# The scan of a bidirectional RWKV-7 mixer on one core: inverse loads and row stores go to GpSimd's queue, low parts to GpSimd

## The chip, the core and the metric

The kernel runs on one core of a Trainium2 chip. Its time is the device time of one launch in microseconds (us). The kernel before took 1601.57 us (median of 3 runs, 1601.06 to 1603.18). A core has TensorE (PE in the profile, with its weight loads as PEld), VectorE (DVE), ScalarE (ACT), GpSimd (POOL) and SyncE (SP), each working through its own instructions in order. DMA transfers are issued as instructions of SP, ACT or POOL; a transfer that waits for its data holds whatever stands behind it on the engine that issues it.

## The reference

One layer over 128 context tokens and 2048 latent tokens, width 1024. What matters for the change:

```python
h = _rmsnorm(x, lp['norm_g']) * (1.0 + scale) + shift
proj = h @ lp['w_in']
r, k, v, g_a, b_gate, c_gate, u_conv, g_b = jnp.split(proj, IN_SPLITS, axis=-1)
...
def step(S, inp):                      # per token, per direction, per head
    r_t, w_t, k_t, v_t, kk_t, a_t = inp
    s_kk = jnp.einsum('bdhij,bdhj->bdhi', S, kk_t)
    S = (S * w_t[..., None, :] - s_kk[..., :, None] * (kk_t * a_t)[..., None, :]
         + v_t[..., :, None] * k_t[..., None, :])
    return S, jnp.einsum('bdhij,bdhj->bdhi', S, r_t)
...
ya = ya.astype(x.dtype) * jax.nn.silu(g_a)                                        # group A: the scan
yb = b_gate * _short_conv(c_gate * u_conv, lp['conv_w'], is_latent) * jax.nn.silu(g_b)   # group B
u = jnp.concatenate([ya, yb], axis=-1) @ lp['w_out']
return x + gate * u, s_final           # then a last RMS norm
```

## The kernel before

There are three phases. Phase 1 projects the tokens in blocks of 384 and leaves per-token operands of the scan in scratch arrays in HBM (`at`, `lo`, `ops`, `vt`, `q`, `sg`, and `mixT`, the transposed input of the output projection, whose lower half is group B's result). Phase 2 is the scan. Phase 3 is the output projection with the last norm; part of its work, the products of group B with the output weights, is used to fill TensorE during the scan.

**The scan.** A chunk has 64 tokens. A *stage* is 8 chunks of a head pair in each of the two directions; there are 17 stages, number 0 to 16. For each stage the delta rule needs inverses of 32x32 triangles. They are made by GpSimd: `load_I` (L947) fetches the triangles from `at` with four transfers of 128 KB (L956) into a tile `ab`, of which there are two; `solve_steps` (L963) does the elimination in 15 steps of one multiplication (L978, into `ztmp`) and two subtractions (L981, into `zt`), after a preparation (L970 `dgp`, L971, L973, L974), and stores the result in `zt` in HBM (L986), from where the stage fetches it as `zc` (L1058). Stages 0 to 5 are solved before the main loop begins; the main loop's round s computes stage s, prepares stage s + 1 and asks for the solve of stage s + 7 (`partI`, L1354). GpSimd so makes the inverses of stages 6 to 16 one after the other during the scan.

**The other work in a round.** `finish` (L1209) normalises a head pair of 512 tokens once both directions are summed, gates it and writes it into 128 rows of `mixT` (L1262; L1260 for the context): the *mixed rows*. `conv_weights` (L1415) fetches the output weights of group B, and `split` (L1407) cuts each into a high part (ScalarE, L1409) and a low part, the difference (L1410); the low part is `wol`. `conv_split` (L1442) does the same for a tile of 128 tokens of group B (`mhc`; its low part is the second half of the tile, two tiles exist). `fill` (L1466) multiplies these on TensorE for nine of the 17 token tiles (`AHEAD`), half a tile of 512 columns per round, four groups of three products: high by high, high by low weight, low mix by high weight. The sums stand in the one PSUM tile `psa`, are copied by ScalarE to a tile `z0` (L1475) and stored in HBM (L1476): the *added products*, which phase 3 fetches again. The tile `z0` has one buffer, and so has `psa`:

```python
z = O.r.tile([128, 512], F32, tag="z0", name=f"z0_{i}{h}", bufs=1)
P.copy(z[:], ps[:])
```

so the copy of one half cannot begin before the store of the half before it has landed, and the products of the half after cannot begin before the copy is done.

**What sets the order.** The rounds' order on TensorE is written out by hand (`ORDER`, L758) and pinned product by product. Everything else is placed by the framework's scheduler, which estimates when each instruction could run and writes one fixed order for each engine; on the chip an engine follows that order, and waits at an instruction until its semaphores are reached. `behind` (L848) adds an order without a wait. `O.line` is true from the start of the main loop until its last round.

Of the kernel before, what the change touches and what calls it, by code (L numbers as in the profile page):

```python
# [36 lines left out]
def place(d, h):  # L37

    x = 1 - h if d == 0 else h
    return slice(x * 64, x * 64 + 64)  # L40
# [721 lines left out]
def phase2(K):  # L762
    nc, tc, A, S = K.nc, K.tc, K.A, K.S
    V, G, P, T = nc.vector, nc.gpsimd, nc.scalar, nc.tensor
    D = nc.sync.dma_start
    B = Ctx()
    O = Ctx()
# [32 lines left out]
    def spare(name, dt, tag, n=1024):  # L800

        pool = O.rI if tag in ("ab", "zt", "ztmp") else O.l1 if tag in ("ab2", "a1", "a2", "o10", "o11") else O.r0
        return pool.tile([128, n], dt, tag=tag, name=name, bufs=dict(F=4, zt=2).get(tag, 1))
# [29 lines left out]
    def ps_tile(shape, name):  # L833

        O.n += 1
        if O.pm is None and O.p2 is None:
            return K.rest_tile(name)
        if O.pm is not None and (O.n % 5 < 2 or O.p2 is None):
            return O.pm.tile(shape, F32, tag="m", name=name)
        return O.p2.tile(shape, F32, tag="s", name=name)  # L840
# [7 lines left out]
    def behind(r, ins):  # L848

        if ins is not None:  # L850
            tc.add_manual_dep(r.ins, ins.name, mybir.DependencyInfo(mybir.DependencyClass.NoSync, mybir.DependencyReason.DATA), reason="order")
# [13 lines left out]
    def now(r):  # L865
        if O.line:
            behind(r, O.last)

    def scaled(r):
        if O.line:  # L870
            behind(r, O.scaled)

    def tr(dst, src, one, after):
        r = T.transpose(dst, src, one)
        if O.line:
            behind(r, O.last)
            O.last = r.ins
        else:
            behind(r, after)

    def tl(shape, tag, b, pool=None, dt=F32):
        return (pool or O.l0).tile(shape, dt, tag=tag, name=f"{tag}_{K.u()}", bufs=b)
# [64 lines left out]
    def load_I(s, ab, after):  # L947

        for gi, (d, units, blk) in enumerate(stages[s]):
            for h in range(2):  # L950
                dst = ab[h * 64 + gi * 32:h * 64 + gi * 32 + 32].rearrange("p j i -> p (j i)")
                if blk is None:
                    src = S["at"][d, :, 0:2].rearrange("p u s b j i -> p (u s b) (j i)")
                else:
                    src = S["at"][d, units[0][0], units[0][1]:units[0][1] + 8].rearrange("u s b j i -> (u s b) (j i)")
                behind(D(dst, src), after)  # L956

    def solve(*a):

# [249 lines left out]
    def finish(p, blk, y):  # L1209

        t0 = NCTX + 512 * blk if blk is not None else 0
        other = p == 3 and blk in (2, 3)
        place = lambda tag: spare(f"{tag}{K.u()}", F32, "ztmp" if tag == "sg" else "zt", 512) if other else tl([128, 512], tag, 1)
        sg, q = place("sg"), place("yo")
        if blk is None:
            parts = [(pp_, slice(pp_ * 128, pp_ * 128 + 128)) for pp_ in range(4)]
        else:
            parts = [(p, slice(0, 512))]

        def fetch(nm, t_):  # L1220
            if blk is None:
                D(t_[:].rearrange("p (g t) -> p g t", t=128), S[nm][:, 0:128].rearrange("(g p) t -> p g t", p=128))
            else:
                now(D(t_[:], S[nm][p * 128:(p + 1) * 128, t0:t0 + 512]))

        fetch("sg", sg)
        fetch("q", q)
        yield
        heads = lambda x: x.rearrange("p q (h v) -> p (q h) v", h=2)
        per_head = lambda x: x[:].unsqueeze(2).broadcast_to((128, 8, 64))  # L1230
        if blk is None:
            mn = tl([128, 8], "ymn", 1)
            V.tensor_reduce(mn[:], heads(y[:]), mybir.AxisListType.X, ALU.add)
            V.scalar_tensor_tensor(heads(y[:]), per_head(mn), -1.0 / 64, heads(y[:]), ALU.mult, ALU.add)
        w = place("w")
        w4 = w[:].rearrange("p (q v) -> p q v", q=4)
        now(P.activation(w4, y[:], AF.Square))
        yield
        ss = tl([128, 8], "yss", 2)
        scaled(V.tensor_reduce(ss[:], heads(w4), mybir.AxisListType.X, ALU.add))  # L1240
        P.activation(ss[:], ss[:], AF.Sqrt, bias=B.geps[:], scale=1.0 / 64)
        yield
        V.reciprocal(ss[:], ss[:])
        V.tensor_tensor(heads(y[:]), heads(y[:]), per_head(ss), ALU.mult)
        yield
        pt = ps_tile([128, 512], f"psT{K.u()}")
        for i in range(4):
            if blk is None:
                dst = pt[:, i * 128:i * 128 + 128]
            else:  # L1250
                dst = pt[:].rearrange("p (m q t) -> p m q t", m=2, q=4)[:, :, i]
            tr(dst, y[:, i], B.idt[:], K.reached)
        yield
        o = y[:].rearrange("p q t -> p (q t)")
        for g_, cs in parts:
            scaled(V.scalar_tensor_tensor(o[:, cs], pt[:, cs], B.gwh[:, g_:g_ + 1], sg[:, cs], ALU.mult, ALU.mult))
        yield
        scaled(V.tensor_tensor(o, o, q[:], ALU.add))
        if blk is None:
            D(S["mixT"][0:512, 0:128].rearrange("(g p) t -> p g t", p=128), o.rearrange("p (g t) -> p g t", t=128))  # L1260
        else:
            D(S["mixT"][p * 128:(p + 1) * 128, t0:t0 + 512], o)  # L1262
        K.mixed[blk] = K.mixed.get(blk, 0) + 1
        yield

# [130 lines left out]
def phase3(K):  # L1396
    nc, tc, A, S = K.nc, K.tc, K.A, K.S
    V, G, P, T = nc.vector, nc.gpsimd, nc.scalar, nc.tensor
    D = nc.sync.dma_start
    O = Ctx()  # L1400
# [3 lines left out]
    HALF = [slice(0, 512), slice(512, 1024)]  # L1404
    wk, ready, cm, am = {}, {}, {}, {}

    def split(hi, lo, raw, eng, at=K_NOW):  # L1407

        at(K, P.copy(hi, raw))  # L1409
        at(K, eng.tensor_tensor(lo, raw, hi.bitcast(F32), ALU.subtract))  # L1410
# [4 lines left out]
    def conv_weights():  # L1415
        raw = {}

        def load(k):
            raw[k] = O.r.tile([128, 1024], F32, tag="mhc", name=f"woraw{k}", bufs=2)
            for c in HALF:  # L1420
                K.now(D(raw[k][:, c], A["wout"][k * 128:(k + 1) * 128, c]))
                yield

        def cut(k):
            t = [O.r.tile([128, 1024], F32R, name=f"wo{x}{k}") for x in "hl"]
            wk[k] = [[x[:, c] for c in HALF] for x in t]
            for n, c in enumerate(HALF):
                split(wk[k][0][n], wk[k][1][n], raw[k][:, c], V)
                yield

        k0, k1, k2, k3 = CONV
        for step in (load(k0), load(k1), cut(k0), load(k2), cut(k1), load(k3), cut(k2), cut(k3)):
            yield from step
# [8 lines left out]
    def conv_split(i, at=K_NOW):  # L1442
        raw = cm[i]
        t = O.r.tile([128, 1024], F32R, tag="mhc", name=f"mhc{i}", bufs=2)
        cm[i] = [t[:, c] for c in HALF]
        split(*cm[i], raw[:], V, at)

    def mixes():
        for i in AHEAD:
# [5 lines left out]
    def product(ps, m, ks, h, n, start, stop, pin=lambda r: None):  # L1455

        hi, lo = m
        wh, wl = [x[h] for x in wk[ks[n]]]
        c = slice(n * 128, n * 128 + 128)
        for x, (l, r) in enumerate(((hi, wh), (hi, wl), (lo, wh))):  # L1460
            r = T.matmul(ps[:], l[:, c], r, start=start and n == x == 0, stop=stop and n == 3 and x == 2)  # L1461
            O.first = O.first or r.ins
            K.reached = r.ins
            pin(r)

    def fill():  # L1466

        for i in AHEAD:
            for h in range(2):
                ps = K.fill_tile(f"psa{i}_{h}")  # L1470
                for n in range(4):
                    product(ps, cm[i], CONV, h, n, True, True, K.pin)
                    if n == 3:
                        z = O.r.tile([128, 512], F32, tag="z0", name=f"z0_{i}{h}", bufs=1)
                        P.copy(z[:], ps[:])  # L1475
                        P.dma_start(S["z0"][i, :, HALF[h]], z[:])  # L1476
                    yield

    def att_weights():
# [127 lines left out]

    O.first = K.reached = None
    K.weights, K.conv_weights, K.mixes, K.fill, K.att_weights, K.first_mixes, K.tail = weights, conv_weights, mixes, fill, att_weights, first_mixes, tail
    K.open_rest, K.rest_tile, K.close_rest = open_rest, rest_tile, close_rest  # L1610

# [48 lines left out]
```

## Time and profile before

| | |
|---|---|
| time, median of 3 runs | 1601.57 us (1601.06 to 1603.18) |
| the profiled execution's own time | 1599.22 us |
| its span, first to last instruction | 1597.2 us |
| the main loop of the scan in it, about | 1010 to 1440 us |
| DMA issues on POOL's queue in all | 15 (L986) |
| DMA issues on SP's queue in all | 991 |

The profile comes from one execution; its times count from the span's start. "Busy" leaves out waiting and the issuing of DMAs by SP and ACT; a DMA issue on POOL is a row of its own with a duration. The idle time before an instruction is put down to what released it last. Of a DMA the profile has the issue and the landing.

### The profile page before, as it was taken

The page shows a single profiled execution, that of the slowest core. Times are in us where ns is not written, and L with a number is a line of the kernel's source. Part 1 is how long each engine was busy: PE and PEld are TensorE (multiplying, and loading weights), DVE is VectorE, ACT ScalarE, POOL GpSimd, SP SyncE. Part 2 cuts the span into 40 slices and gives each one's busy share as a digit, 9 for nine tenths or more (in the row PEclk, how much of TensorE's full clock was granted, in tenths as well). Part 3 has the DMA queues.
Part 4 walks back from the last instruction along what each step waited for, and adds up shares of the span by engine and source line. Part 5 has one row for each costly group of instructions (what it writes and reads, how often), then busy time and mean ns, then how long its engine had stood idle before and what let it go on. Part 6 is the DMA issues. An engine that isn't in the chain of part 4 may idle for free.

```text
span 1597.2 us, 42430 instructions
## 1 busy us (share of the span) xinstructions
PE 1510.8 (95%) x17160; PEld 1383.8 (87%) x17160; DVE 1126.1 (71%) x2246; ACT 772.9 (48%) x1645; POOL 584.5 (37%) x1030
## 2 busy tenths in 40 slices
PE   5899999999999999999989989988999899989997
PEld 2799988999999999999989889887888788877886
DVE  5875978795746875747878787567577576667773
ACT  4554655462515453525544301576756667663331
POOL 0011212120202121202286466388888883012431
PEclk8899999999999999999999999999999999999999
DMA  9587758766555656564675865787767686658751
GB/s 375 193 298 225 265 185 307 254 226 224 173 173 161 218 184 220 158 194 171 226 241 184 281 212 175 199 224 204 198 187 189 183 224 172 172 164 290 260 175 66
DMA packets 242354, 336.66 MB, mean 211 GB/s; under 512 B 91688, under 2 KB 192296, under 8 KB 228080
## 3 DMA queue, kind: packets, MB, share of 16 engines
q1 hardware_dynamic: 233616, 323.27, 63.9%
q10 hardware_dynamic: 7344, 6.76, 1.3%
q0 software_dynamic: 1200, 3.93, 0.7%
q8 instruction: 135, 2.21, 0.6%
q14 instruction: 59, 0.48, 0.1%
HBM read 212.64 MB, written 121.26 MB: 209 GB/s over the span
## 4 chain that ended last, share of the span: by engine, by line
PE 45%; DVE 11%; DMA 5%; POOL 5%; issue 3%; ACT 3%; SPq 0%; ACTq 0%; DVEq 0%; POOLq 0%
PE psu L1461 8%; PE psE L855 4%; PE psS L855 3%; PE psa L1461 2%; POOL zt L981 2%; POOL ztmp L978 2%; PE psF L855 1%; DVE fg L981 1%; PE psX L855 1%; PE psG L855 1%; PE mmv L166 1%; PE mmv L167 1%; PE mmv L168 1%; PE mmg L168 1%; PE mmg L167 1%
## 5 line engine op out<-in xcount | busy, mean ns | idle before, releaser
L981 POOL TENSOR_TENSOR zt<-zt,ztmp 128x30 f32<-128x30 f32 (+7 forms) x390 | 156.6, 402 | 30.6
L855 PE MATMUL psE<-fg 128*64 128x128 f32 x2176 | 152.5, 283 | 7.2 <-ACT fg L1085 5.4
L855 PEld LDWEIGHTS psE<-fg 128*64 128x64 f32 x2176 | 125.3, 143 | 11.5 <-ACT fg L1085 6.9
L329 POOL TENSOR_TENSOR shk<-rawl 128x384 f32<-128x384 f32 (+1 forms) x24 | 24.9, 1039 | 243.1 <-ACT rawl L325 243.0
L855 PE MATMUL psS<-sv,E 128*64 128x64 f32 x2176 | 96.1, 230 | 14.9 <-DVE sv L1184 10.1
L855 PEld LDWEIGHTS psS<-sv,E 128*64 128x64 f32 x2176 | 80.8, 141 | 29.3 <-DVE sv L1184 17.9
L846 ACT COPY E<-psE 128x256 f32<-128x256 f32 x136 | 49.4, 373 | 101.0 <-DVE E L1147 88.9
L1080 DVE TENSOR_TENSOR fg<-psG,consts 64x256 f32<-64x256 f32 x136 | 57.4, 422 | 54.1 <-PE psG L855 52.1
L978 POOL TENSOR_TENSOR ztmp<-ab,zt 128x60 f32<-128x60 f32 (+4 forms) x165 | 88.2, 534 | 12.9
L844 ACT ACTIVATE fg<-psX 64x512 f32<-64x512 f32 x136 | 80.5, 592 | 24.0 <-PE psX L855 21.6
L1461 PE MATMUL psu<-woh,mha 128*128 128x512 f32 x272 | 89.0, 396 | 0.3 <-DVE mha L1410 0.3
L1147 DVE TENSOR_TENSOR E<-psE,consts 128x256 f32<-128x256 f32 x136 | 56.6, 416 | 37.4 <-PE psE L855 36.3
L329 POOL TENSOR_TENSOR shv<-rawl 128x384 f32<-128x384 f32 (+1 forms) x24 | 21.8, 909 | 166.8 <-ACT rawl L325 166.6
L1585 POOL TENSOR_TENSOR z<-z,x 128x512 f32<-128x512 f32 x32 | 46.8, 1463 | 93.9 <-DVE z L1581 43.1
L1085 ACT COPY fg<-psG 64x256 f32<-64x256 f32 x136 | 49.8, 366 | 57.9 <-DVE fg L1080 19.5
L1184 DVE TENSOR_TENSOR sv<-psS,pc 64x128 f32<-64x128 f32 x262 | 65.1, 276 | 13.3 <-PE psS L855 11.4
L446 POOL COPY pcs<-pp 128x6 f32<-128x6 f32 (+1 forms) x48 | 21.3, 445 | 137.7 <-ACT pp L435 137.4
L166 PE MATMUL mmc<-h,w 128*128 128x384 f32 (+1 forms) x192 | 64.5, 336 | 5.9 <-ACT q1r L327 4.1
L166 PE MATMUL mmg<-h,w 128*128 128x384 f32 (+1 forms) x192 | 64.2, 334 | 3.8 <-ACT q1v L327 3.8
L166 PE MATMUL mmgb<-h,w 128*128 128x384 f32 (+1 forms) x192 | 64.0, 333 | 1.2 <-DMA w<-scr_wsp 0.8
L166 PE MATMUL mmb<-h,w 128*128 128x384 f32 (+1 forms) x192 | 62.9, 328 | 1.5 <-ACT ta L439 1.5
L1586 ACT ACTIVATE x<-z 128x512 f32<-128x512 f32 x34 | 21.5, 632 | 88.3 <-POOL z L1585 79.8
(316 smaller groups left out, 5125.6 us busy)
## 6 DMA issues: line engine op xcount, KB each, us to landing
w<-scr_wsp SPq DMA_DIRECT2D x68, 1024.0 KB, 6.1
scr_wsp<-w SPq DMA_DIRECT2D x34, 1024.0 KB, 4.9
scr_ops<-pair SPq DMA_DIRECT2D x80, 384.0 KB, 3.8
wr<-in_win SPq DMA_DIRECT2D x34, 512.0 KB, 5.9
o<-scr_ops SPq DMA_DIRECT2D x32, 512.0 KB, 5.1
fg<-scr_ops SPq DMA_DIRECT2D x120, 128.0 KB, 4.8
x<-in_x SPq DMA_DIRECT2D x17, 512.0 KB, 3.8
wadas<-in_wada SPq DMA_DIRECT2D x8, 1024.0 KB, 13.6
```

The source lines that it names most:

```text
L166: T.matmul(ps[:, :n], w[:, 0, k], hh[:, 0, k, :n], start=k == 0, stop=False)
L844: P.activation(dst, src, AF.Copy, scale=-1.0)
L846: P.copy(dst, src)
L855: r = T.matmul(*a, start=True, stop=True, **k)
L978: eng.tensor_tensor(tv, ab[:, j:j + 2, j + 2:32].unsqueeze(1).broadcast_to((128, kn, 2, n)), zt[:, :kn, j:j + 2].unsqueeze(3).broadcast_to ...
L981: last = eng.tensor_tensor(zt[:, :kn, j + 2:32], zt[:, :kn, j + 2:32], tv[:, :, r], ALU.subtract).ins
L1080: m = V.tensor_tensor(g.gs[H[1 - h], g.op, h, us], ps[gi][r, :, 64:128], B.mG[r, g.d].unsqueeze(1).broadcast_to((64, 4, 64)), ALU.mult)
L1085: st.copied = P.copy(g.gs[H[1 - h], 0, h, us], ps[gi][r, :, 0:64])
L1147: V.tensor_tensor(to(H[1]), of(H[1]), B.mE[:, g.d].unsqueeze(1).broadcast_to((128, 4, 64)), ALU.mult)
L1184: r = V.tensor_tensor(dst, sp[gi][0:64, q], B.pc[0:64, d, 2 * p:2 * p + 2, c:c + 1].broadcast_to((64, 2, 64)), ALU.mult)
L1461: r = T.matmul(ps[:], l[:, c], r, start=start and n == x == 0, stop=stop and n == 3 and x == 2)
L1585: (V if last else G).tensor_tensor(z[:, cs], z[:, cs], xt[:, cs], ALU.add)
```

## The change

Three transfers change their queue and two subtractions their engine; what is computed stays the same.

- The loads of the triangles in the main loop (L956, 44 of them, for stages 6 to 16) are issued by GpSimd instead of SP.
- The stores of mixed rows (L1260 and L1262, 17) are issued by GpSimd instead of SP.
- The stores of the added products (L1476, 18) are issued by GpSimd instead of ScalarE.
- The low parts of group B's weights (`wol`, L1410, 8) and of the mixes that the rounds prepare (`mhc`, L1410, 9 of 17) are subtracted by GpSimd instead of VectorE.

```diff
@@ load_I
-                behind(D(dst, src), after)
+                behind((G.dma_start if O.line else D)(dst, src), after)
@@ finish
         scaled(V.tensor_tensor(o, o, q[:], ALU.add))
         if blk is None:
-            D(S["mixT"][0:512, 0:128].rearrange("(g p) t -> p g t", p=128), o.rearrange("p (g t) -> p g t", t=128))
+            G.dma_start(S["mixT"][0:512, 0:128].rearrange("(g p) t -> p g t", p=128), o.rearrange("p (g t) -> p g t", t=128))
         else:
-            D(S["mixT"][p * 128:(p + 1) * 128, t0:t0 + 512], o)
+            G.dma_start(S["mixT"][p * 128:(p + 1) * 128, t0:t0 + 512], o)
@@ conv_weights
             for n, c in enumerate(HALF):
-                split(wk[k][0][n], wk[k][1][n], raw[k][:, c], V)
+                split(wk[k][0][n], wk[k][1][n], raw[k][:, c], G)
@@ conv_split
-        split(*cm[i], raw[:], V, at)
+        split(*cm[i], raw[:], V if at is not K_NOW else G, at)
@@ fill
                         P.copy(z[:], ps[:])
-                        P.dma_start(S["z0"][i, :, HALF[h]], z[:])
+                        G.dma_start(S["z0"][i, :, HALF[h]], z[:])
```

How this moves instructions is seen in each engine's order. TensorE's is the same in both kernels. First GpSimd, where the main loop's first solve (stage 6) follows the last one of the time before it (`zt_10569`, stage 5); `ab_11007`, `zt_11012` and `dgp_11014` belong to stage 6:

```order
 L986 DMA scr_zt<-zt_10569 128x512
 L968 MEMSET zt_11012 64x16 x2
+L956 DMA ab_11007<-scr_at 32x1024 x4
 L970 COPY dgp_11014<-ab_11007 128x16
 L971 TENSOR_SCALAR zt_11012<-dgp_11014 64x16
```

The loads stand right behind the store of the solve before, on the engine that needs them. Before, they stood on SP, behind the operands of later stages:

```order
 L911 DMA o_9816<-scr_ops_58 128x2x512
 L918 DMA a_10980<-scr_lo 128x256 x2
-L956 DMA ab_11007<-scr_at 32x1024 x4
 L1018 DMA sv_11167<-scr_vt 64x1024
 L1018 DMA sv_11169<-scr_vt 64x1024
```

SP now goes from one fetch to the next there. Last, GpSimd late in the scan, in the solve of stage 16 (`zt_16101`, `ztmp_16102`, `ab_16096`), the last one; `mhc_16420` is token tile 9, `z_81_16477` the second half of the added products of tile 8, `y_13325` mixed rows:

```order
 L978 TENSOR_TENSOR ztmp_16102<-ab_16096,zt_16101 128x220
+L1410 TENSOR_TENSOR mhc_16420<-mxc_15909,mhc_16420 128x512
 L981 TENSOR_TENSOR zt_16101<-zt_16101,ztmp_16102 128x5x22 x2
 L978 TENSOR_TENSOR ztmp_16102<-ab_16096,zt_16101 128x240
 L981 TENSOR_TENSOR zt_16101<-zt_16101,ztmp_16102 128x6x20 x2
```

The low part of tile 9 has moved into the fifth step of the last solve. In the same way the stores of added products, of mixed rows and the next loads stand in the middle of the solves, about one set in each solve of stages 9 to 16. GpSimd's order from the stage-6 loads to this subtraction holds ten whole solves (stages 6 to 15), 44 loads, 8 weights' low parts, 5 mixes' low parts (tiles 5 to 9), 7 stores of added products and 7 of mixed rows.

## The prediction

> **What bounds the kernel now.** First the busy time by stage, to see which engine is full where (the columns are named in the first row):
>
> ```profile
> core 0: us, PE busy (x) PEld busy (x) DVE busy (x) ACT busy (x) POOL busy (x), PEclk, DMA share, GB/s
> 0.00:1000.00 1000.00, 951.51 (x6718) 906.50 (x6719) 729.10 (x1352) 440.31 (x926) 257.66 (x402) 0.98 0.66 221
> 1000.00:1440.00 440.00, 410.62 (x9726) 358.38 (x9725) 293.97 (x734) 286.87 (x603) 280.06 (x596) 0.97 0.71 192
> 1440.00:1597.00 157.00, 148.63 (x720) 118.93 (x718) 102.99 (x161) 45.72 (x117) 46.78 (x32) 0.98 0.58 201
> ...
> 1240.00:1280.00 40.00, 34.51 (x842) 29.80 (x832) 21.29 (x56) 24.55 (x52) 34.59 (x79) 0.91 0.64 176
> ```
>
> TensorE is the bound: in the scan (second row) it idles 29.4 of 440 us, and that is all that any change of queues there can win. GpSimd is idle for 160 us of the 440, but not evenly. In the 40 us of the last row it is busy for 34.59 us and TensorE has one of its few holes, 5.5 us. Second, GpSimd's order of time around its first and in its last solve of the main loop:
>
> ```profile
> 986.90 0.61 POOL L986 DMA_DIRECT2D scr_zt<-zt  x1
> 987.52 0.31 POOL L968 MEMSET zt<- 64x16 f32 x2
> 1022.92 0.20 POOL L970 COPY dgp<-ab 128x16 f32<-128x16 f32 x1 [35.09 <-DMA ab<-scr_at]
> ...
> 1313.84 0.56 POOL L978 TENSOR_TENSOR ztmp<-ab,zt 128x220 f32<-128x220 f32 x1
> 1314.48 0.89 POOL L981 TENSOR_TENSOR zt<-zt,ztmp 128x110 f32<-128x110 f32 x2
> ...
> 1321.32 0.62 POOL L978 TENSOR_TENSOR ztmp<-ab,zt 128x252 f32<-128x252 f32 x1
> ...
> 1332.83 0.61 POOL L986 DMA_DIRECT2D scr_zt<-zt  x1 [0.30 <-POOL zt L981]
> ```
>
> From 1022.92 to 1332.83 GpSimd makes eleven inverses without a pause, 28.2 us each (309.9 / 11). A round of the scan takes about 25.5 us (17 in some 433 us), so GpSimd is slower than the rounds; it can be, because nobody waits for it soon. The last inverse is stored at 1332.83 and fetched only here:
>
> ```profile
> 1381.49 1.33 SPq L1058 DMA_DIRECT2D zc<-scr_zt  x2
> ```
>
> So GpSimd is 49 us ahead at the end. This lead is what the kernel lives on, and only the inverses are asked of it. Third, what SP waits for:
>
> ```profile
> SPq L1262 <- DVE E L1147: 46.0, 12, 8.4
> ...
> SPq L956 <- POOL zt L981: 21.1, 7, 8.0
> ...
> 1246.98 2.71 SPq L956 DMA_DIRECT2D ab<-scr_at  x4
> ...
> 1256.85 2.33 SPq L1058 DMA_DIRECT2D zc<-scr_zt  x2
> ```
>
> (total us, times, longest). SP stands before a store of mixed rows 46 us and before the triangles' loads 21 us in all, and fetches behind them are late; the hole of TensorE just named lies behind one of these (the loads could go at 1246.98, the inverse behind them at 1256.85).
>
> **The change part by part.** *Removed.* VectorE loses 17 subtractions, ScalarE 18 issues, SP 77 issues and both waits above. VectorE and ScalarE are not full in the scan (294 and 287 of 440 us), so their part shortens no path by itself; I take it as 0. SP's is worth at most the 29.4 us of holes, and probably the one of 5.5 us.
>
> *Start of the solves.* GpSimd is idle from 987.8 to 1022.92 because SP reaches the first loads late:
>
> ```profile
> 1016.50 3.02 SPq L956 DMA_DIRECT2D ab<-scr_at  x4
> ...
> L385 SPq DMA_DIRECT2D scr_at<-stages x16: 382/505/1001, 751.1 to 906.9; - x16
> ```
>
> The triangles were stored from 906.9 us on at the latest, so GpSimd can issue its four loads at 987.8. With 0.61 us an issue (the row 986.90), the last goes at 989.7, lands some 4 us later (below), and the solve of stage 6 begins at 993.7 instead of 1022.92: 29.2 us of lead won.
>
> *Added to GpSimd*, up to the low part of token tile 9 in the last solve:
>
> ```profile
> L986 POOL DMA_DIRECT2D scr_zt<-zt x13: 614/614/617, 957.7 to 1332.8; - x13
> ...
> DMA to landing us min/median/max: 2.2/4.4/8.4
> ...
> L956 SPq DMA_DIRECT2D ab<-scr_at x44: 302/419/1565, 1016.5 to 1276.2; - x44
> ...
> DMA to landing us min/median/max: 2.4/3.9/6.7
> ...
> L1410 DVE TENSOR_TENSOR mhc<-mxc,mhc x17: 671/692/1789, 1082.1 to 1565.1; 128x512 fp32r<-128x512 f32 x17
> L1410 POOL TENSOR_TENSOR wol<-woraw,woh x8: 1258/1276/1556, 1382.7 to 1438.1; 128x512 fp32r<-128x512 f32 x8
> ```
>
> (durations in ns: min/median/max.) The 13 subtractions cost GpSimd 1.276 us each, the last row (the same operation and shape as VectorE's 0.692): 16.6 us. The issues are 40 loads (stages 7 to 16), 7 stores of added products and 7 of mixed rows, 54 in all. The profile has no load on POOL's queue. Its stores take 0.614 us each, in an extreme 0.756 (before the scan); the same loads on SP take at least 0.302. I take 0.614, the only row of this queue: 33.2 us, with 16.3 and 40.8 as the ends. A new wait comes with the loads: the copy L970 of the next solve is put into the solve before, some 2 to 4 us of work behind the last of the four issues, and holds all of GpSimd until they land. With a landing of 4.0 us (between 3.9 for these loads and 4.4 for POOL's stores) and the place of each copy in the order, it comes to about 1.4 us for each of ten, 14 us; the ends are 0 (all land in 2.4 us) and 41 (6.7 us: 2.7 more for each).
>
> The work that stays, from 1022.92 to the multiplication behind which the subtraction stands (1314.48, where the next row begins), is 291.5 us. So GpSimd ends the low part of tile 9 at 993.7 + 291.5 + 16.6 + 33.2 + 14 = 1349.0.
>
> *Who waits for it.* TensorE needs it in the third product of tile 9:
>
> ```profile
> 1296.85 0.50 PE L1461 MATMUL psa<-woh,mhc 128*128 128x512 f32 x1
> 1297.19 0.40 PE L1461 MATMUL psa<-wol,mhc 128*128 128x512 f32 x1
> 1297.43 0.62 PE L1461 MATMUL psa<-woh,mhc 128*128 128x512 f32 x2
> ...
> 1311.96 0.57 ACT L1475 COPY z<-psa 128x512 f32<-128x512 f32 x1
> ```
>
> It starts at 1297.43 before, and cannot start before 1349.0: 51.6 us late, and TensorE's order is fixed, so all behind it is late. The stores say the same: the copy at 1311.96 (first half of tile 9) must find the single tile `z0` free, whose store stands four steps further on in GpSimd's order (behind a row that ended at 1321.94): 993.7 + (1321.94 - 1022.92) + 16.6 + 33.2 + 14 = 1356.5, landed by 1360.5, 48.6 us late. Before, this store had no solve in front of it. By the same sum GpSimd is in time at first: tile 5's low part (8 weights and one mix) ends some 6 us late, and a store of added products may lie some 20 us behind its copy (a round less copy, issue and landing) before it holds the next. Each round costs GpSimd 28.2 + 6 issues (3.7) + half a subtraction (0.6) + 1.4 = 33.9 us against 25.5, so the lead goes by 8 us a round, and from about stage 12's solve the rounds run at GpSimd's pace. What is late next is everything: inverses come after it in the same order, but they are not needed sooner. After the last solve GpSimd's own work is thin, and TensorE runs at its old pace with the lag.
>
> *Given back.* Behind 1297 little is idle on TensorE:
>
> ```profile
> 1400.00:1440.00 40.00, 35.53 (x682) 30.04 (x681) 24.77 (x63) 25.48 (x54) 7.81 (x6) 0.96 0.50 146
> ```
>
> Of these 4.5 us I give back 2, because SP has fetched ahead by then. The sum for the profiled execution: 1597.2 + 51.6 - 2 = 1646.8 of span, with the 2.0 us around it (1599.22) 1648.8. Its time lies 2.35 us under the median of the runs, so the median goes to 1651.
>
> A rule of the Trainium skill speaks to the hope behind such a move: "DMA: Bandwidth & Descriptors", section "Issuing engines are not separate DMA queues", says that transfers from any engine share the same 16 DMA engines and that spreading them saves only the issuing sequencer's time. By it the transfers gain nothing, the 2 us given back fall away, and the sum would be 1653. The same page ("Anatomy of one DMA") puts a POOL transfer at 2.0 us and its bytes at 436 GB/s, an estimate of 2.3 us for 128 KB; the rows above have 3.9 and 4.4, and I go by them. By the page the loads' wait would shrink to near nothing and the start come 1.7 us sooner, up to 16 us less: 1635.
>
> **The rivals.** *Cheap issues.* If GpSimd issues in 0.302 us and the loads land in 2.4, 16.9 us, 14 us of waits and 1.6 us at the start fall away: 32.5 less, 1619. For it: SP's rows. Against it: thirteen rows of POOL's queue within 3 ns.
>
> *Dearer issues or landings.* At 6.7 us for the landing, the waits grow by 27 and the start by 2.7, at 0.756 an issue by 7.6: 37 more, 1688. For it: single landings of POOL's stores at 8.4 us, and four issues in a row that no trace shows on this queue. Against it: the medians.
>
> *No early start.* If something holds the first loads as SP's queue did, the start stays at 1022.92, the 29.2 us won are lost, and the end is 1680. For it: the order says only what stands where. Against it: the triangles are stored by 906.9, and GpSimd has nothing between.
>
> *Not slower: GpSimd keeps its lead.* At 993.7 + 291.5 = 1285.2 GpSimd would be 12.2 us ahead of the product at 1297.43. If all that is added came to under 12.2 us, nothing would wait, and the hole of 5.5 us behind SP's waits would close: 1601.6 - 5.5 = 1596. It decides at 12.2 us; the subtractions alone are 16.6, so it needs issues beside the work and subtractions at half their row. For it speaks only that solves spread by 1 us with what VectorE does beside them, and VectorE does less.
>
> **How the numbers follow.** The forecast (1635 to 1667) has 0.6; cheap issues (1608 to 1635) 0.18; dearer ones and no early start (above 1667) together 0.15; GpSimd keeping its lead 0.07, of which 0.05 faster. The likeliest is 1651. The range from 1617 to 1676 leaves out the far ends of the cheap and dear cases and the last rival, about 2 in 10. About 0.2% (3 us) is what a measurement of this kernel can tell from none. Faster by more than that 0.05, within it 0.02, slower 0.93.
>
> **What would show it.** In the changed profile: the first copy L970 of the scan near 994 with its wait before it gone; solves 33 to 34 us apart instead of 28.2 from stage 9 on, GpSimd busy without a hole until some 1365; ScalarE's copies L1475 and TensorE's `psa` products waiting for GpSimd (stores of `z0`, low parts of `mhc`) in the rounds between 1200 and 1365, and TensorE's idle time in the scan up from 29 to some 80 us; SP's waits before L1262 and L956 gone; the stage behind the scan as long as before. I am wrong if POOL's loads take under 0.3 or over 0.8 us each, if the copies L970 wait for none of them, or if TensorE waits in the scan for something other than GpSimd.

## The result and the profile after

The changed kernel takes 1665.57 us (median of 4 runs, 1657.47 to 1672.23) against 1601.32 us before (now 4 runs): 1.040 of its time, 95% interval 1.035 to 1.044. It is slower by 64 us, as forecast (1651, range 1617 to 1676), though 15 us further. The profiled execution took 1663.88 us with a span of 1662.1 us; its numbers follow. One run of e12 below (1830.37 us, at a granted clock of 0.752 where all others had at least 0.957) is left out of its number.

First the windows around the scan's main loop: of the changed kernel, up to 1500 us and up to 1515, and (second fence) of the kernel before up to 1450, which is 65 us, the whole loss, ahead of 1515. They have the columns of the prediction's first fence (stretch, length, busy time of PE, PEld, DVE, ACT and POOL, granted clock, DMA share, GB/s):

```profile
980.00:1500.00 520.00, 435.58 (x9869) 380.84 (x9867) 296.03 (x743) 286.31 (x602) 336.50 (x703) 0.92 0.63 169
980.00:1515.00 535.00, 450.58 (x9995) 392.16 (x9994) 306.27 (x768) 290.30 (x611) 341.87 (x708) 0.93 0.63 172
```

```profile
980.00:1450.00 470.00, 439.81 (x9981) 384.26 (x9979) 314.12 (x783) 289.84 (x610) 287.30 (x616) 0.97 0.71 195
```

TensorE idles 84.4 us instead of 30.2, in either window. Up to 1515 it has done the same work (9995 products, 9981 before) and was busy for 450.6 us instead of 439.8. So the 65 us are some 54 of new idle time and some 11 of products that took longer; the last section has a reason for part of the 11. What ends the idle time is in TensorE's order of time in the changed kernel:

```profile
1102.50 1.22 PE L1461 MATMUL psa<-woh,mhc 128*128 128x512 f32 x2 [6.76 <-POOL mhc L1410]
...
1226.37 1.22 PE L1461 MATMUL psa<-woh,mhc 128*128 128x512 f32 x2 [18.25 <-POOL mhc L1410]
...
1292.83 1.22 PE L1461 MATMUL psa<-woh,mhc 128*128 128x512 f32 x2 [12.14 <-POOL mhc L1410]
...
1359.58 1.22 PE L1461 MATMUL psa<-woh,mhc 128*128 128x512 f32 x2 [12.13 <-POOL mhc L1410]
```

Four times TensorE stands before the third product of a token tile (5, 7, 8, 9) until GpSimd has made the tile's low part, 49.3 us in all. The last of these products began at 1297.43 before; it is 62.15 us late, and the span is 64.9 us longer. Behind it nothing more is lost to speak of.

GpSimd in the changed kernel, at the start of its eleven solves and at the low part of tile 9 (order of time), and then what it waits for between 985 and 1400 us (total, times, longest):

```profile
987.13 1.97 POOL L956 DMA_DIRECT2D ab<-scr_at  x4
998.83 0.20 POOL L970 COPY dgp<-ab 128x16 f32<-128x16 f32 x1 [9.73 <-DMA ab<-scr_at]
...
1111.53 0.62 POOL L986 DMA_DIRECT2D scr_zt<-zt  x1
...
1348.79 0.60 POOL L986 DMA_DIRECT2D scr_zt<-zt  x1
...
1358.27 1.26 POOL L1410 TENSOR_TENSOR mhc<-mxc,mhc 128x512 fp32r<-128x512 f32 x1
```

```profile
POOL dgp L970 <- DMA ab<-scr_at: 40.6, 10, 9.7
POOL mhc L1410 <- ACT mhc L1409: 13.7, 1, 13.7
POOL wol L1410 <- ACT woh L1409: 4.1, 1, 4.1
```

The solve of stage 6 begins at 998.8 instead of 1022.9; between the stores at 1111.53 and 1348.79 lie seven solves, 33.9 us each instead of 28.2. Up to tile 9's low part GpSimd waits for nothing but the loads it issued itself and, once, for a weight's high part (the 13.7 us come after it). The chain that sets the end is GpSimd's own order.

### The profile page after: what moved, and what is told of

The parts are those of the page before. It is cut to its first block, busy times and chain, and to the rows that moved or that the text cites. A ratio compares the mean times of both kernels' runs of the same rounds, so it can differ in the third digit from the quotient of the medians.

```text
span 1662.1 us, 42482 instructions
## 1 busy us (share of the span) xinstructions
PE 1521.7 (92%) x17160; PEld 1390.2 (84%) x17160; DVE 1118.9 (67%) x2229; ACT 773.0 (47%) x1645; POOL 638.0 (38%) x1126
## 4 chain that ended last, share of the span: by engine, by line
PE 39%; POOL 13%; DVE 11%; DMA 6%; issue 3%; ACT 2%; SPq 0%; DVEq 0%; ACTq 0%; POOLq 0%
PE psu L1461 8%; POOL zt L981 5%; POOL ztmp L978 3%; PE psE L855 3%; DMA ab<-scr_at 3%; PE psS L855 2%; PE psa L1461 2%; DVE fg L981 1%; PE psF L855 1%; PE psX L855 1%; DMA scr_mixT<-ob 1%; PE mmv L166 1%; PE psG L855 1%; PE mmg L168 1%; PE mmg L166 1%
## 5 line engine op out<-in xcount | busy, mean ns | idle before, releaser
L855 PE MATMUL psE<-fg 128*64 128x128 f32 x2176 | 148.8, 280 | 11.6 <-ACT fg L1085 6.3
L1461 PE MATMUL psa<-woh,mhc 128*128 128x512 f32 x144 | 58.7, 446 | 49.3 <-POOL mhc L1410 49.3
L1461 PEld LDWEIGHTS psa<-woh,mhc 128*128 128x128 f32 x144 | 28.0, 198 | 61.2 <-POOL mhc L1410 51.0
```

Source lines behind the costliest of these rows:

```text
L855: r = T.matmul(*a, start=True, stop=True, **k)
```

## The experiments

All of them are compared with runs of the kernel before on the same chip, whose median lay between 1598.6 and 1600.2 us. The changed kernel itself was not run beside them: what an experiment "brings back" is counted from its 1665.57 us, whose four runs spread over 15 us, and is sure to a few us only. The changed kernel's edits have short names here: *loads* (L956), *rows* (stores of mixed rows, L1260 and L1262), *products* (stores of the added products, L1476), *weights* and *mixes* (low parts, L1428 and L1446).

### One tie, or two

The prediction named two places at which TensorE hangs on GpSimd: the low parts of the mixes, and the single tile `z0` behind the stores of added products. The first three runs take each of them away, and both.

```diff
 e1: the changed kernel, mixes back
-        split(*cm[i], raw[:], V if at is not K_NOW else G, at)
+        split(*cm[i], raw[:], V, at)
 e2: the changed kernel, products back
-                        G.dma_start(S["z0"][i, :, HALF[h]], z[:])
+                        P.dma_start(S["z0"][i, :, HALF[h]], z[:])
 e3: both
```

> The changed kernel, but the low parts of the mixes (mhc) are subtracted by VectorE again; loads, stores of mixed rows and of added products, and the weights' low parts stay on GpSimd. Theory A (GpSimd's one fixed order is the slow chain, and the low parts and the stores of added products are two separate places at which TensorE is tied to it): TensorE's waits for mhc (49 us in the changed kernel's trace) vanish, but the tie over z0 stays: the store of z0_81 began at 1366.2; five subtractions of 1.27 us fewer and one solve step (1.7) later put it at about 1361.5, landed at 1365.9, where the copy behind it stood at 1312.0 before: +54, so 1655 us (1643 to 1665). Theory B (the low parts alone are the cause, TensorE waits for nothing else): 1665.6 - 49 = 1617 us or less.

Measured: 1654.85 us (1.034, interval 1.032 to 1.037). The time is the one that theory A gave (1655). TensorE's waits for the low parts are gone, and two other waits stand in their place, on ScalarE (985 to 1440 us):

```profile
ACT y L846 <- DMA scr_mixT<-y: 33.2, 2, 19.4
ACT z L1475 <- DMA scr_z<-z: 28.0, 4, 11.3
```

In the kernel before neither wait is there at all. Theory B (the low parts alone) falls: only 11 us came back of the 49 that TensorE had waited for them. The second row is the tie over `z0`, from which the 1655 was worked out. The first row is larger and was not in the prediction, so it is in part luck that the number was met so closely.

> The changed kernel, but the stores of the added products are issued by ScalarE again. Theory A: the low part of tile 9 ended at 1359.5 in the changed kernel; seven stores of 0.63 us fewer (4.4) and one step later (1.7): 1356.8, against 1297.4 before: +59, so 1660 us (1648 to 1670). Theory C (the single tile z0, held by late stores, is the cause): 1605 to 1620 us.

Measured: 1671.61 us (1.045, 1.043 to 1.047), just above the expected margin (1648 to 1670) and no better than the whole change. Theory C falls. The excess over 1660 has a likely reason in one row, though no run tests it: without the stores the next solve's loads moved to the end of a solve, right ahead of the copy that needs them, and GpSimd's waits for their landing (985 to 1400 us) grew from 40.6 us to

```profile
POOL dgp L970 <- DMA ab<-scr_at: 51.6, 10, 10.5
```

> The changed kernel with both ties cut: low parts of the mixes on VectorE, stores of added products on ScalarE; the loads, the stores of mixed rows and the weights' low parts stay on GpSimd. Theory A: GpSimd is still slower than the rounds, but only inverses (49 us of lead before) and mixed rows are asked of it, so nearly all of the loss goes: 1600 to 1612 us (the weights' last low part ends near 1101, some 13 us behind TensorE's first use of it at 1087.7 before, of which 5 to 10 may stay). Theory D (something that this edit leaves alone is the cause, as the loads on GpSimd's queue or the clock): 1640 us or more.

Measured: 1649.63 us (1.031, 1.028 to 1.033). **This was a miss**: with both named ties cut, 49 of the 64 us are still lost. Three views of the same place, ScalarE, GpSimd and TensorE in order of time:

```profile
1274.49 0.58 ACT L846 COPY y<-psS 64x512 f32<-64x512 f32 x1 [8.58 <-DMA scr_mixT<-y]
1305.51 0.58 ACT L846 COPY y<-psS 64x512 f32<-64x512 f32 x1 [30.44 <-DMA scr_mixT<-y]
```

```profile
1303.06 0.63 POOL L1262 DMA_DIRECT2D scr_mixT<-y  x1
```

```profile
1306.54 1.99 PE L855 MATMUL psG<-fg,o 64*64 64x128 f32 x32 [36.46 <-ACT E L846]
```

GpSimd comes to a store of mixed rows at 1303.06, late, because it stands near the end of a solve. Only when it has landed may ScalarE copy the next partial sums into that tile `y` (there are six). ScalarE stands there for 30.44 us, everything behind the copy in its order stands too, and TensorE is empty for 36.46 us. The stores of mixed rows are a third tie, through the buffers of `y`.

### The loads, and all ties cut

```diff
 e4: the changed kernel, loads back
-                behind((G.dma_start if O.line else D)(dst, src), after)
+                behind(D(dst, src), after)
 e5: the kernel before, with loads and weights alone on GpSimd
```

> The changed kernel, but the triangles are loaded by SP again (no issue of loads and no wait for their landing in GpSimd's order, and no early start). Theory A: the first solve begins at 1022.9 again; 280 us of solve work, 5 for three later steps, 16.5 of subtractions, 8.5 of 14 stores: the low part of tile 9 at 1333 against 1297.4, +36: 1637 us (1625 to 1648). Theory E (the loads are the whole loss: 20 us of issues and 31 to 41 us of landings): 1600 to 1612 us. Theory B and C both expect nearly no gain here: 1655 or more.

Measured: 1645.86 us (1.029, 1.027 to 1.031), 9 us over the number, inside the margin of theory A. The loads are worth some 20 us of the 64; theory E, that they are all of it, falls.

> The kernel before with two parts of the change: the triangles' loads and the weights' low parts on GpSimd; stores of mixed rows on SP, of added products on ScalarE, low parts of the mixes on VectorE. Theory A2 (three ties, the stores of mixed rows being the third: in the run with the other two cut, ScalarE stood 53.9 us before a tile y whose store was late): with all three cut only inverses are asked of GpSimd. Eleven solves at 33.3 us from 998.8 and eight subtractions end at about 1375, stored by 1380, against the fetch at 1381.5 before: just in time. 1600 us (1595 to 1610). Theory D2 (loads on GpSimd's queue cost by themselves, by their issues or by transfers that disturb others): 1630 or more, as 20 us came back when they alone were taken off.

Measured: 1602.76 us against 1598.63 (1.002, 1.001 to 1.004; 10 runs). With three ties cut the loss is gone but for 4 us, though the loads cost GpSimd the same as ever. Its stores of inverses (ns, first and last start), and then GpSimd's wait for landings and SP's for an inverse (985 to 1440 us):

```profile
L986 POOL DMA_DIRECT2D scr_zt<-zt x13: 586/630/665, 955.9 to 1380.4; - x13
```

```profile
POOL dgp L970 <- DMA ab<-scr_at: 50.8, 10, 9.6
...
SPq L1058 <- DMA scr_zt<-zt: 9.1, 2, 7.4
```

GpSimd waits 50.8 us for its loads and nobody minds: the last inverse is stored at 1380.4 instead of 1332.8, just when SP wants it (1381.5 before). The lead of 49 us has been spent to the end, and it is the lead that had hidden this work. Time on GpSimd's order costs next to nothing as long as only inverses are asked of it and the lead lasts; here it just did.

### Each tie alone

If the cause is the place in GpSimd's order and not the amount of work, one tie must cost clearly more than the time that it adds to GpSimd, without the other parts. The kernel before, with one part of the change each:

```diff
 e6: rows (L1262; L1260 in the same way)
-            D(S["mixT"][p * 128:(p + 1) * 128, t0:t0 + 512], o)
+            G.dma_start(S["mixT"][p * 128:(p + 1) * 128, t0:t0 + 512], o)
 e7: products
-                        P.dma_start(S["z0"][i, :, HALF[h]], z[:])
+                        G.dma_start(S["z0"][i, :, HALF[h]], z[:])
 e8: mixes
-        split(*cm[i], raw[:], V, at)
+        split(*cm[i], raw[:], V if at is not K_NOW else G, at)
```

> The kernel before with one part of the change: the stores of mixed rows on GpSimd. In GpSimd's order each now stands between two solves; the one of y_998 behind the last solve, at 1333, against 1292.9 on SP before: 40 us late. Theory A2: the run without the other ties bore such a store 78 us later with an end 48 us later, so some 30 us of lateness are free (six tiles y), and 10 us are paid, less the 5.5 us hole that SP's waits caused: 1605 us (1597 to 1612). Theory F (the 46 us of SP's waits were worth something and the tiles y are enough): 1592 to 1597 us.

> The kernel before with one part of the change: the stores of the added products on GpSimd. Theory A2: the store of z0_81 stands behind 13 steps of the last solve, 1328.5 before; with seven stores (4.4) 1333, landed at 1336.7, while the copy behind it stood at 1312.0: 25 us, 1625 us (1613 to 1640; more if GpSimd itself waits for the copies). Theory G (one part alone is harmless; only the sum of the change outruns GpSimd's lead of 49 us): 1598 to 1604 us.

> The kernel before with one part of the change: the low parts of the mixes on GpSimd. Theory A2: the one of tile 9 stands behind eight steps of the last solve, 1319.5 before; with five subtractions (6.3) 1326 against the product at 1297.4: 28 us, 1629 us (1618 to 1640). Theory G: 1598 to 1604 us.

Measured: rows 1617.41 us (1.012, 1.009 to 1.015), products 1619.12 (1.012, 1.010 to 1.015), mixes 1623.40 (1.016, 1.013 to 1.018). Each has its own wait, in this order (985 to 1440 us each):

```profile
ACT y L846 <- DMA scr_mixT<-y: 35.4, 2, 21.1
```

```profile
ACT z L1475 <- DMA scr_z<-z: 47.0, 7, 9.1
```

```profile
PE psa L1461 <- POOL mhc L1410: 36.2, 4, 20.0
```

Theory G (one part alone is harmless) falls three times: seventeen stores of half a microsecond cost 19 us, eighteen others 20 us, nine subtractions 25 us. By their rows they add 9, 10 and 11 us to GpSimd's work (0.54, 0.56 and 1.26 us each), half of what they cost; and e5, whose loads add 22 us of issues and 50.8 us of waits, cost 4. What is paid is how late they stand, behind solves of 28 us. For products and mixes the position gave the size (1625 and 1629 expected). For rows it did not, and **that was a miss**: 1605 was expected, 1612 at most. The expectation went by the store at 1333, but ScalarE stood before the landings of two earlier ones, issued at 1160.6 and 1274.4: 21.1 and 14.3 us. The three losses (18.8, 20.5, 24.8) sum to 64, and so does the change, but that is chance: e4 holds all three and loses 46, while the loads bring the other 20 only because the ties are there (e5).

### The waits for the landing

In the changed kernel the loads are issued a few microseconds ahead of the copy that needs them. Their place comes from an order behind a late instruction of the round. Without it they stand where their tile comes free, at the end of the solve before last:

```diff
 e9: the changed kernel
-                behind((G.dma_start if O.line else D)(dst, src), after)
+                behind((G.dma_start if O.line else D)(dst, src), None if O.line else after)
 e10: the kernel before, with this line alone
```

> The changed kernel with its four parts, but the loads of the triangles are no longer ordered behind a late instruction of the round; in GpSimd's order they now stand at the end of the solve before last, where their tile comes free, a whole solve (28 us) ahead of the copy that needs them. Takes away the waits for the landing (40.6 us in the changed kernel's trace, one of them, 9.7, before the first solve) and nothing of the added work. Theory A2: eleven solves of 28.2, 44 loads, 15 stores of 0.6 and some 12 subtractions of 1.27 from 986 end at 1342 with the low part of tile 9, against 1297.4 before: +40 to +45, minus what the solves ran faster (11 us) : 1632 to 1647, say 1638 us. Theory H (GpSimd stands before stores whose data are late anyway, so that a wait taken away comes back there): 1655 us or more.

Measured: 1662.63 us (1.039, 1.037 to 1.042), against the 1638 of theory A2: **a miss**. Theory H gave the number, but not the reason: GpSimd waits before no store until the solves are over. Its waits up to 1358 us, and its order of time where the last solve ends:

```profile
POOL dgp L970 <- DMA ab<-scr_at: 17.4, 6, 4.4
```

```profile
1356.94 0.58 POOL L986 DMA_DIRECT2D scr_zt<-zt  x1 [0.30 <-POOL zt L981]
1357.54 1.29 POOL L1410 TENSOR_TENSOR mhc<-mxc,mhc 128x512 fp32r<-128x512 f32 x1
```

The same store in the changed kernel:

```profile
1377.78 0.58 POOL L986 DMA_DIRECT2D scr_zt<-zt  x1 [0.30 <-POOL zt L981]
```

The waits fell from 40.6 to 17.4 us and the last solve ended 20.8 us sooner. But the scheduler's new order has the low part of tile 9 behind the whole last solve instead of in its fifth step. It is made at 1357.54 instead of 1358.27. What the edit won was given back by the order that it changed. No run puts the low part back into the fifth step of these earlier solves.

> The kernel before with the triangles' loads alone on GpSimd, a whole solve ahead. Theory A2: only inverses are asked of GpSimd; it ends the last at about 1305 (986 + 11 x 28.2 + 22 of issues, minus some), earlier than before (1332.8), and waits for nothing. SP loses its 21 us of waits before L956 and with them the hole of 5.5 us: 1594 us (1591 to 1599). Theory D2 (loads on GpSimd's queue disturb by themselves): 1603 or more. The holes are worth nothing: 1599 to 1602.

Measured: 1590.57 us against 1598.67 (0.993, interval 0.991 to 0.996): **faster than both kernels**, and just past the fast end of the expected range (1591 to 1599). SP's waits in its profiled execution (985 to 1440 us) no longer have the 21.1 us before L956; those before L1262 are still there. Then its windows by stage, and GpSimd's stores of inverses:

```profile
SPq L1262 <- DVE E L1147: 58.5, 13, 8.1
```

```profile
0.00:1000.00 1000.00, 955.29 (x6735) 909.94 (x6736) 723.23 (x1358) 441.70 (x930) 253.94 (x397) 0.99 0.66 221
1000.00:1440.00 440.00, 413.19 (x9768) 360.34 (x9766) 294.59 (x739) 286.78 (x601) 300.70 (x646) 0.97 0.71 194
...
1240.00:1280.00 40.00, 36.02 (x812) 31.66 (x809) 22.88 (x60) 24.67 (x52) 32.22 (x70) 0.87 0.58 148
```

```profile
L986 POOL DMA_DIRECT2D scr_zt<-zt x13: 592/595/627, 961.0 to 1342.9; - x13
```

Where TensorE won the 8 us is not settled. That execution (1593.71 us, the longest of its six) shows TensorE 3.8 us more busy up to 1000 us (955.29 against 951.51) and 2.6 us more in the 440 us after (413.19 against 410.62). Of its 17160 products the 7000th begins at 1013.6 instead of 1017.1 and the 16500th at 1440.3 instead of 1444.9, so most of the gain was there when the loop had hardly begun; but e6, whose loads stayed on SP, has its 7000th at 1014.0. The hole between 1240 and 1280, which the prediction put behind SP's waits, is smaller and not gone (36.02 us busy of 40, before 34.51). Nor did GpSimd wait for nothing and end earlier, as was expected: it waited 14.4 us for its loads (seven times), its last inverse was stored at 1342.9 instead of 1332.8, and that harmed nobody. Nor is it shown which half of the edit won. In e5 the loads are on GpSimd too, at their old place and beside the weights, SP has none of the 21.1 us either, and nothing was won; the loads a solve ahead on SP's queue were not run.

### What SP's other waits are worth

```diff
 e11: the kernel before (L1262 only)
-            D(S["mixT"][p * 128:(p + 1) * 128, t0:t0 + 512], o)
+            P.dma_start(S["mixT"][p * 128:(p + 1) * 128, t0:t0 + 512], o)
 e12: e10 with this line too
```

> The kernel before with the stores of mixed rows issued by ScalarE, where each stands between two copies of E; SP's 46 us of waits before L1262 go, and GpSimd has no part in it. If SP's waits cost TensorE something: 1593 to 1598 us. If SP's waits are hidden: 1599 to 1602. If ScalarE waits for VectorE at each store (up to 8.4 us before on SP, which comes to it sooner): above 1603.

> Both of the edits before: loads of the triangles on GpSimd a whole solve ahead, stores of mixed rows on ScalarE; SP has no wait of either kind. Theory A2 with SP's waits worth their hole: 1590 to 1596 us, the fastest of all. If they are hidden: as the better of the two runs with one edit each.

Measured: e11 1597.58 us against 1598.67 (0.999, 0.998 to 1.001; 12 runs): no change. (By its time alone it would fall under "cost TensorE something", but the range for hidden waits, 1599 to 1602, begins above the kernel before's own 1598.67.) e12 1586.17 us (five runs, 1585.21 to 1593.48; 0.993, 0.991 to 0.996): the same as e10, and a little under the expected 1590 to 1596. SP's 46 us of waits before the stores of mixed rows, its longest item, are hidden: taking them off SP is worth nothing when ScalarE issues the stores. SP does not come free by it either: in e11 its waits before L956 are 35.0 us instead of 21.1.

## Why the prediction was right, and where it was not

The direction, the chain and the range were right; the sum was 10.5 us short at tile 9 and 15 us at the end. That it came so near is in part luck: three terms were 26 us too small together, two were 15.5 us too large. Its terms, up to the low part of tile 9, from these groups of the changed kernel (ns: min/median/max):

```profile
L956 POOL DMA_DIRECT2D ab<-scr_at x44: 489/503/627, 987.1 to 1343.2; - x44
...
DMA to landing us min/median/max: 2.5/4.4/10.2
...
L1476 POOL DMA_DIRECT2D scr_z<-z x18: 539/560/639, 1127.8 to 1522.0; - x18
...
L1262 POOL DMA_DIRECT2D scr_mixT<-y x16: 539/569/582, 1132.3 to 1540.5; - x16
...
L1410 POOL TENSOR_TENSOR mhc<-mxc,mhc x9: 1261/1267/1289, 1101.2 to 1486.2; 128x512 fp32r<-128x512 f32 x9
```

| term | predicted, us | measured, us |
|---|---|---|
| start of the first solve | 993.7 | 998.8 |
| work that was there before | 291.5 | 280.0 |
| 13 subtractions | 16.6 | 16.5 |
| 54 issues | 33.2 | 29.2 |
| waits for landings (ten solves) | 14 | 30.9 |
| wait for a weight's high part | none | 4.1 |
| low part of tile 9 ends | 1349.0 | 1359.5 |

The measured terms are sums over GpSimd's rows between 998.83 and 1359.53 (40 loads 20.7, seven stores of each kind 4.4 and 4.1); the landings are the 40.6 us above without the 9.73 ahead of the first solve, and the work is what remains.

- **The landing waits are the term that was mis-sized most**, 14 forecast, 30.9 paid, and 5 more at the start. The step "with a landing of 4.0 us ... about 1.4 us for each of ten" took a median landing (they came out at 4.4) for what is the last of four loads to land: the fourth load of the first solve landed 10.1 us after its issue, and those of the ten others 5.5 us on average (2.5 to 8.1). These 1.5 us more than 4.0, ten times, are most of the error. The far bound, 6.7 us a landing and 41 us in all, came nearer than the median. The Trainium skill's formula in "DMA: Bandwidth & Descriptors", section "Anatomy of one DMA", gave an estimate of 2.3 us for such a load; the trace does not agree (4.4 us, from 2.5 to 10.2), and the 1635 us that followed from it was the wrong way to lean.
- **Issues**: 0.50 us for a load, 0.54 to 0.64 for a store; the one row taken (0.614) was dear by 4 us in all. The rival "cheap issues" (0.302) falls, and so do the dearer ones (0.756); of "dearer issues or landings" the landings came by more than half.
- **The old work took 11.5 us less** than before. Not all of it is faster work: the rows of the same 547 instructions sum to 248.8 us instead of 253.9; 3 us are shorter gaps between them, and 3 us are rows of issues that overlap the row before. VectorE was busy 57% of the scan's time instead of 67% (296.03 of 520, 314.12 of 470). No run tests whether that is the cause of the 5 us; the prediction had named it as a possibility and given it no number.
- **The early start** was there (rival "no early start" falls), 5 us less of it because the first four loads landed late.
- **The pace**: 33.9 us a solve was forecast and 33.9 was measured, by luck: the waits were dearer and the rest cheaper. TensorE's idle time was to be some 80 us; it was 84.4.
- **Given back**: minus 2 us was forecast behind tile 9, plus 2.7 came (64.9 of span against 62.15 there).
- **The ties**: the step "Who waits for it" named the low parts and the stores of added products. Both are real, and each alone costs 20 us or more (e7, e8). In the changed kernel itself the one over `z0` hardly shows: ScalarE waits 10.8 us for it, in two waits, since TensorE is held by the low parts already. With these back on VectorE it comes out (28.0 us in e1). The prediction had the stores of mixed rows down as time on GpSimd and nothing else; e3 and e6 show the third tie. This made no difference to the number, since the sum went by the low part of tile 9, and all the difference to what would repair the kernel: the prediction's account would have led to e3, at 1650.
- **SP's waits**: "SP's is worth at most the 29.4 us of holes, and probably the one of 5.5 us" is met in size by the 8 us of e10, but the mechanism is not shown: the hole itself stayed in part, and e5 won nothing. For the waits that looked larger it was wrong (0 in e11). SP lost 61 issues (991 before, 930 after), not 77; no term used that number.
- **GpSimd keeps its lead** (rival, 0.07): it falls for the change. e5 shows how much the lead can carry: loads and weights spend all of it, and next to nothing is paid, since only inverses are asked of GpSimd behind them.
- **Another queue**: with the stores of mixed rows on ScalarE's queue instead of SP's the time stayed the same (0.999, e11). This agrees with the rule of the Trainium skill, "DMA: Bandwidth & Descriptors", section "Issuing engines are not separate DMA queues", that another engine saves only the issuing sequencer's time. On GpSimd the saving is a cost: here an issue is a row of half a microsecond in the order of the engine that computes.

## What to carry to other kernels

An engine that is off the critical path and slower than the loop lives on a lead, and whatever is put into its order inherits its lateness: before moving a store or a small operation there, ask not how long it takes but behind what it will stand, and which buffer or operand somebody else waits for. Cutting one such tie shows little while another holds (of 64 us e1 brought back 11, e2 nothing, both together 16), so cut them all once (e5) before judging any. Loads on GpSimd's queue a whole solve ahead of their use, with the stores left where they were, made this kernel faster (e10, 0.993); a few microseconds ahead, and with the weights beside them, they did not (e5, 1.002).

## What was not expected of the hardware

After each long wait TensorE runs at half its clock for some microseconds. The changed kernel behind the wait that ended at 1359.58 (columns as above; the third number from the end is the granted clock):

```profile
1359.58:1361.58 2.00, 2.00 (x4) 1.16 (x4) 0.00 (x0) 0.00 (x0) 1.75 (x4) 0.50 0.00 0
1361.58:1363.58 2.00, 2.00 (x55) 1.82 (x56) 0.24 (x1) 0.00 (x0) 1.70 (x4) 0.68 0.03 8
1363.58:1365.58 2.00, 2.00 (x84) 1.96 (x78) 1.91 (x7) 1.13 (x4) 1.76 (x4) 1.00 0.18 41
```

The granted clock is 0.50 in the first two microseconds, 0.68 in the next two, then 1.00; the two products at 1359.58 take 1.22 us together, as do those behind the other three waits, where two took 0.62 before (1297.43 in the prediction). This agrees with the Trainium skill, "TensorE: Matmul & The Clock Gate", section "Part 1: The HAM clock gate", by which an idle window of about 3.4 us brings the clock to half until a busy one has passed. The loss is 2 x 0.50 + 2 x 0.32 = 1.6 us of full clock for this wait. Behind the other three the granted clock is 0.50 over the first 3.2 us too, so an estimate for all four is some 6 us of the 11 that the products took longer. The first three of these should not add to the time: up to tile 9 GpSimd waits for nothing from TensorE, so the next low part comes no later, and TensorE waits that much less for it. The 1.6 us behind the last wait may be part of the 2.7 us that the prediction had as minus 2.

The same subtraction of 128x512 takes 1.27 us on GpSimd and 0.69 on VectorE, 1.83 times as long, and that was as forecast. That 50.8 us of waits on an engine can go with a loss of 4 us (e5), and seventeen stores of some 0.54 us with one of 19 us (e6), was not.
